# A two-layer attention decoder on one core: small TensorE work handed out between the big matmuls, attention units one per step, memory loads on a second queue

## The chip, the cores and the metric

One core of a Trainium2 chip runs the whole program. The metric is the device time in microseconds, median of three runs. TensorE (PE) multiplies; its weight loads stand in the profile as an engine of their own, PEld. ScalarE (ACT) and VectorE (DVE) read the products, GpSimd (POOL) works on SBUF only, SyncE (SP) issues nearly all transfers. In the matmul rows, "128*128 128x512" is an array use of 128 rows by 128 columns and a moving operand of 512 columns.

## What is computed

256 tokens of width 1024 pass two layers. Each layer normalises, projects, attends in three ways and merges. All is float32.

```python
for l in range(2):
    h = rmsnorm(x, norm_g[l]); z = h @ w_in[l]              # 1024 -> 7968
    o_a = nsa(nsa_q, nsa_kv, gate, compress weights) * silu(nsa_silu)   # 8 heads of 64, 2 kv groups
    o_b = fox(fox_qkv, fox_f, ...) * silu(fox_silu)                     # 8 heads of 64, forget gate
    o_m = memory_xattn(mem_q, rmsnorm(mem) @ w_mem_kv[l]) * silu(mem_silu)   # 4 heads of 128
    u = g0 * (o_a @ w_branch_a) + g1 * (o_b @ w_branch_b) + g2 * (o_m @ w_branch_m)
    x = x + u @ w_out[l]
```

## The kernel before

**Big matmuls.** Every weight matrix is streamed in pieces of 256 rows by up to 512 columns (`stream`). `load_w` issues a piece's transfer into `wraw` (4 buffers); `split_w` splits it into a high part on ACT (L168) and a low part on DVE (L169), 3 buffers each. `gemm_steps` (L233 to L235) multiplies one piece: for two token blocks and two row blocks three matmuls of 512 columns (high*high, low*high, high*low), 12 in all; this is a **step**, and a projection has four. `silu_path_T` (L769 to L772) is a step with 24 matmuls of 256 columns. A projection accumulates in PSUM banks of the tag "mm" (3 buffers). The projections run in the order `ORDER`.

**Small work.** After each step `tick()` advances a clock. Everything that follows a projection (norms, rotary embedding, transposes through PSUM tag "T" with 2 buffers, splits of the transposed result) is queued with `later(d, fn)` and traced d ticks on. Attention is cut into **units**: `scores` (matmuls into PSUM tag "S", 2 buffers, then mask, max, exp, sum, and the multiply by 1/sum on POOL, L496), one `unit_step` later `transpose` (L502), one later `product` (L453, into tag "O", 1 buffer). A layer has 4 + 8 NSA units (`Unit` in `nsa_units`, token block 0 and 1), a `Cmp` unit after each of these two groups (the compressed branch, L879 and L911), 8 fox units (L1043, L1045) and 4 memory units (L1109). A unit starts only when its `deps` are marked, and a unit that may not start blocks the units behind it. `tick()` makes four unit steps.

**The narrow matmuls.** `compress_in` (L662) gathers the compress rows with 8 float32 products of a 128x64 weight against a 64-column selector, twice a layer; the trace shows each as two instructions. `compress_out` (L793 and on) has a few more narrow ones. `compress_step` runs between the steps of FK and takes an "S" bank for two steps.

**Order.** A scheduler of the language, with a timeline of its own, lays out each engine's instructions: what is traced earlier goes first, once it is ready on that timeline. The engines then run that order.

**The start.** 8 matmuls on zeros (`WARM`, L275), the gains' transpose (L297), the transposes of the memory's first quarter of columns (L363), then the first step of memory keys. SP issues, in this order, memory quarter 0, weight piece 0 in two halves, quarter 1, piece 1, quarter 2, piece 2, quarter 3, then x.

Of the kernel before, what the change touches and what calls it, by code (L numbers as in the profile page):

```python
# [26 lines left out]
WARM = 8  # L27

ORDER = "K2 K1 Q SA SB FK MG FQ FV SM MQ".split()
# [30 lines left out]
def hybrid_kernel(ctx: ExitStack, tc, I, cst_d, out_d):  # L60
# [131 lines left out]

    def tick():
# [23 lines left out]
    def need(k):  # L217
        for _ in range(60):
            if k in done_:
                return  # L220
            tick()
        raise AssertionError(k)

    def gemm_steps(act, pp, g, last, consume):
# [29 lines left out]
    def mem_cols(mrow, g):  # L254

        cs = slice(g * 256, (g + 1) * 256)
        nc.sync.dma_start(mrow[:, :, cs], I["mem"][0].rearrange("(t p) d -> p t d", p=128)[:, :, cs])
# [8 lines left out]
    for g in range(4):  # L266
        mem_cols(mrow0, g)
# [80 lines left out]
    def to_T(dst, src, t, k0, scale=1.0):  # L348

        hi, lo = dst[:2]  # L350
        q = pT()
        for k in range(4):
            nc.tensor.transpose(q[:, k * 128:(k + 1) * 128], src[:, k * 128:(k + 1) * 128], ident)
        ts = slice(t * 128, (t + 1) * 128)
        split_evac(hi[:, k0:k0 + 4, ts], lo[:, k0:k0 + 4, ts], q.rearrange("p (k t) -> p k t", k=4), scale)

    def to_T_scaled(dst, src, g, gain):

        hi, lo = dst[:2]
        q = pT()  # L360
        for k in range(2):
            for t in range(NT):
                nc.tensor.transpose(q[:, (k * 2 + t) * 128:(k * 2 + t + 1) * 128],  # L363
                                    src(t)[:, (g * 2 + k) * 128:(g * 2 + k + 1) * 128], ident)
        for k in range(2):
            kg, s = g * 2 + k, q[:, k * 256:(k + 1) * 256]
            gc = gain[:, kg:kg + 1]
            nc.scalar.activation(hi[:, kg, :], s, AF.Copy, scale=gc)
            nc.vector.scalar_tensor_tensor(lo[:, kg, :], s, gc, hi[:, kg, :].bitcast(F32), op0=ALU.mult, op1=ALU.subtract)  # L369
# [13 lines left out]
    def mem_load():  # L383
        mrow = S([128, NT, D], "big")
        for g in range(4):
            mem_cols(mrow, g)
        return mrow

    def mem_norm(l, mrow):

        mT = act_pair(8, "aT")
        for g in range(4):
            def f(g=g):
                to_T_scaled(mT, lambda t: mrow[:, t, :], g, gk[:, l * 8:l * 8 + 8])
                if g == (3 if l else 0):
                    mark("mem")
# [4 lines left out]
            else:  # L401
                f()
        return mT
# [10 lines left out]
    def mem_kv(l, mT, rm):  # L414
# [3 lines left out]
        def on_k(t, p):  # L418
# [3 lines left out]
            def s1():  # L422
# [3 lines left out]
                def s2():  # L426
                    q = pT()
                    for h in range(4):
                        nc.tensor.transpose(q[:, h * 128:(h + 1) * 128], kn[:, h * 128:(h + 1) * 128], ident)
                    ts = slice(t * 128, (t + 1) * 128)  # L430
                    split_evac(KT[0][:, :, ts], KT[1][:, :, ts], q.rearrange("p (h t) -> p h t", h=4))
# [12 lines left out]
    class Out:  # L444
# [4 lines left out]
        def add(self, cols, lhsT, rhs):  # L449
            first = self.O is None  # L450
            if first:
                self.O = pO()
            nc.tensor.matmul(self.O[0:lhsT.shape[1], cols], lhsT, rhs, start=first, stop=False, skip_group_check=True)  # L453

        def close(self):
            self.left -= 1
            if self.left == 0:
                self.done(self.O)

    class Unit:  # L460
# [9 lines left out]
        def scores(self):  # L470
            sp = pS()
            self.score(sp)
# [26 lines left out]
        def transpose(self):  # L499
            q = pT()  # L500
            for i, b in enumerate(self.order):
                nc.tensor.transpose(q[:, i * 128:(i + 1) * 128], self.P[:, b * 128:(b + 1) * 128], ident)  # L502
            w = 128 * len(self.order)
            self.PT = [S([128, 512], tag, bufs=2, dt=F32R)[:, :w] for tag in ("PTh", "PTl")]
            split_evac(self.PT[0], self.PT[1], q[:, :w])
# [24 lines left out]
    for l in range(2):  # L530
# [76 lines left out]
        def rope_k(t, p, i):  # L607
# [4 lines left out]
            def s1():  # L612
                nc.vector.tensor_tensor(kr, kr, b3(r, 2, 64), op=ALU.mult)

                def s2():
                    q = pT()
                    nc.tensor.transpose(q[:, 0:128], kr.rearrange("p h d -> p (h d)"), ident)
# [7 lines left out]
                    mark(("k", l, i, t))  # L625
                later(2 + t, s2)
# [30 lines left out]
        def compress_in(i):  # L657
            q = pT()
# [13 lines left out]
            def s1():  # L672
                nc.scalar.activation(Lhl[i][:, :, 0:30], L3, AF.Copy)
                nc.vector.tensor_tensor(Lhl[i][:, :, 30:60], L3, Lhl[i][:, :, 0:30].bitcast(F32), op=ALU.subtract)
            later(1, s1)
        def run_k2():
# [43 lines left out]
        def on_q(t, p):  # L720
# [4 lines left out]
            def s1():  # L725
# [5 lines left out]
                def s2():  # L731
                    q = pT()
                    for j in range(4):
# [462 lines left out]
```

## Time and profile before

| | us |
|---|---|
| three runs | 645.84, 646.88, 647.96 (median 646.88) |
| the profiled execution | 646.12 |
| its span, first to last instruction | 644.30 |
| TensorE busy in the span | 627.9 (97%) |
| VectorE busy | 485.3 (75%) |
| ScalarE busy | 391.6 (61%) |
| mean granted clock, share of 2.4 GHz | 0.996 |

Ends of matmuls are modelled, and neighbours overlap, so what a matmul costs is read from the distance of its start to the next start. "[1.97 <-DVE sg L754]" behind a row means that the engine was idle for 1.97 us before it, and what ended the idleness.

### The profile page before, as it was taken

How to read it: one execution, taken by the hardware profiler on the slowest of the kernel's cores; microseconds unless marked ns; L12 is line 12 of the kernel's file. 1: busy time of each engine (PE TensorE's matmuls, PEld its weight loads, DVE VectorE, ACT ScalarE, POOL GpSimd, SP SyncE). 2: the span in 40 equal slices, each digit the busy share in tenths (PEclk: the TensorE clock that was granted, in tenths of full speed). 3: DMA queues.
4: the chain of work that ended last, by engine and by line, in shares of the span. 5: the costliest groups of instructions: out<-in, count | busy, mean ns of one | idle time of the engine just before them, and what ended most of it. 6: DMA issues, size and time to landing. Idle time of an engine off the chain costs nothing.

```text
span 644.3 us, 10311 instructions
## 1 busy us (share of the span) xinstructions
PE 627.9 (97%) x3567; PEld 538.3 (84%) x3567; DVE 485.3 (75%) x849; ACT 391.6 (61%) x822; POOL 173.7 (27%) x232
## 2 busy tenths in 40 slices
PE   7999999999998999999999999999999899999997
PEld 5699997878997888888888989877889788888885
DVE  3678889958986976946677798996799588776463
ACT  5767558655756766544557656785566566665441
POOL 1813403343412310603003141140053032052030
PEclk9999999999999999999999999999999999999999
DMA  8757654865343545445655665656544345545541
GB/s 298 182 151 230 195 159 140 198 201 148 121 131 101 161 142 153 134 162 196 229 179 140 191 194 162 172 156 198 160 127 139 91 134 162 163 131 152 175 161 69
DMA packets 75412, 104.51 MB, mean 162 GB/s; under 512 B 16832, under 2 KB 31456, under 8 KB 75360
## 3 DMA queue, kind: packets, MB, share of 16 engines
q1 hardware_dynamic: 75296, 103.84, 54.7%
q8 instruction: 28, 0.46, 0.3%
q14 instruction: 24, 0.20, 0.1%
q10 hardware_dynamic: 64, 0.02, 0.0%
HBM read 102.78 MB, written 1.05 MB: 161 GB/s over the span
## 4 chain that ended last, share of the span: by engine, by line
PE 91%; DVE 3%; DMA 3%; ACT 1%; issue 1%; SPq 0%; ACTq 0%
PE mm L235 20%; PE mm L233 20%; PE mm L234 20%; PE mm L769 4%; PE mm L771 4%; PE mm L772 4%; PE O L453 3%; PE T L502 3%; PE S L235 2%; PE S L233 2%; PE S L234 2%; DMA wraw<-in_w_mem_kv_dram 1%; DVE wlo L169 1%; DMA big<-in_mem_dram 1%; PE S L1109 1%
## 5 line engine op out<-in xcount | busy, mean ns | idle before, releaser
L169 DVE TENSOR_TENSOR wlo<-wraw,whi 128x1024 fp32r<-128x1024 f32 (+3 forms) x185 | 234.2, 1268 | 96.6 <-ACT whi L168 92.0
L168 ACT ACTIVATE whi<-wraw 128x1024 fp32r<-128x1024 f32 (+3 forms) x185 | 192.0, 1039 | 129.3 <-PE mm L234 66.6
L233 PE MATMUL mm<-whi,aTh 128*128 128x512 f32 (+1 forms) x480 | 190.4, 400 | 4.7 <-DVE sg L754 3.9
L234 PE MATMUL mm<-whi,aTl 128*128 128x512 f32 (+1 forms) x480 | 189.4, 395 | 0.1
L235 PE MATMUL mm<-wlo,aTh 128*128 128x512 f32 (+1 forms) x480 | 184.0, 397 | 2.0 <-DVE wlo L169 2.0
L496 POOL TENSOR_TENSOR P<-P,d 128x512 f32<-128x512 f32 (+1 forms) x64 | 57.3, 909 | 197.6 <-DVE d L492 84.5
L233 PEld LDWEIGHTS mm<-whi,aTh 128*128 128x128 f32 x480 | 90.9, 190 | 22.2 <-DVE sg L754 4.7
L235 PEld LDWEIGHTS mm<-wlo,aTh 128*128 128x128 f32 x480 | 90.8, 190 | 20.1 <-DVE wlo L169 3.7
L234 PEld LDWEIGHTS mm<-whi,aTl 128*128 128x128 f32 x480 | 91.2, 190 | 17.3 <-DVE aTl L369 1.1
L769 PE MATMUL mm<-aTh,whi 128*128 128x256 f32 x192 | 54.8, 286 | 0.0
L771 PE MATMUL mm<-aTl,whi 128*128 128x256 f32 x192 | 54.7, 285 | 0.0
L772 PE MATMUL mm<-aTh,wlo 128*128 128x256 f32 x192 | 54.2, 284 | 0.0
L485 ACT ACTIVATE P<-S,m 128x256 f32<-128x256 f32 (+1 forms) x112 | 47.0, 429 | 9.1 <-DVE m L482 6.4
L1019 POOL TENSOR_TENSOR big<-big,t 128x512 f32<-128x512 f32 x16 | 30.0, 1893 | 60.6 <-DVE t L1018 60.6
L339 ACT ACTIVATE PTh<-T 128x512 fp32r<-128x512 f32 (+1 forms) x48 | 26.9, 563 | 22.8 <-PE T L502 22.3
L233 PE MATMUL mm<-whi,oTh 128*128 128x512 f32 x96 | 38.7, 405 | 0.0
L234 PE MATMUL mm<-whi,oTl 128*128 128x512 f32 x96 | 38.3, 399 | 0.0
L235 PE MATMUL mm<-wlo,oTh 128*128 128x512 f32 x96 | 37.7, 396 | 0.0
L769 PEld LDWEIGHTS mm<-aTh,whi 128*128 128x128 f32 x192 | 36.7, 191 | 0.5
L771 PEld LDWEIGHTS mm<-aTl,whi 128*128 128x128 f32 x192 | 36.6, 191 | 0.2
L772 PEld LDWEIGHTS mm<-aTh,wlo 128*128 128x128 f32 x192 | 36.5, 191 | 0.2
L482 DVE TENSOR_REDUCE m<-S 128x2 f32<-128x512 f32 (+3 forms) x64 | 32.6, 514 | 1.0 <-ACT P L485 0.7
(248 smaller groups left out, 1022.3 us busy)
## 6 DMA issues: line engine op xcount, KB each, us to landing
wraw<-in_w_in_dram SPq DMA_DIRECT2D x112, 512.0 KB, 3.7
wraw<-in_w_out_dram SPq DMA_DIRECT2D x16, 512.0 KB, 3.9
wraw<-in_w_mem_kv_dram SPq DMA_DIRECT2D x15, 512.0 KB, 5.1
wraw<-in_w_branch_a_dram SPq DMA_DIRECT2D x16, 256.0 KB, 4.0
wraw<-in_w_branch_b_dram SPq DMA_DIRECT2D x8, 512.0 KB, 3.6
wraw<-in_w_branch_m_dram SPq DMA_DIRECT2D x8, 512.0 KB, 3.6
wraw<-in_w_in_dram SPq DMA_DIRECT2D x8, 408.0 KB, 3.4
wraw<-in_w_in_dram SPq DMA_DIRECT2D x8, 384.0 KB, 3.6
```

The costliest lines, as they stand in the source:

```text
L168: nc.scalar.activation(wh[:, j, :n], v[:, j, :n], AF.Copy)
L169: nc.vector.tensor_tensor(wl[:, j, :n], v[:, j, :n], wh[:, j, :n].bitcast(F32), op=ALU.subtract)
L233: nc.tensor.matmul(o_, hi[:, kg, ts], wh[:, k, :n], start=(kg == 0), stop=False)
L234: nc.tensor.matmul(o_, lo[:, kg, ts], wh[:, k, :n], start=False, stop=False)
L235: nc.tensor.matmul(o_, hi[:, kg, ts], wl[:, k, :n], start=False, stop=last and k == 1)
L482: nc.vector.tensor_reduce(m[:, n:n + c], heads(sp[:, o_:o_ + w * c], c), axis=AXX, op=ALU.max, negate=True)
L485: nc.scalar.activation(self.P[:, k], sp[:, k], AF.Exp, bias=m[:, n:n + 1], accum_out=d[:, n:n + 1])
L496: nc.gpsimd.tensor_tensor(P3, P3, b3(d[:, n:n + c], c, w), op=ALU.mult)
L769: nc.tensor.matmul(o_, ch, hi[:, kg, :], start=(kg == 0 and j % 2 == 0), stop=False, skip_group_check=True)
L771: nc.tensor.matmul(o_, ch, lo[:, kg, :], start=False, stop=False, skip_group_check=True)
L772: nc.tensor.matmul(o_, cl, hi[:, kg, :], start=False, stop=(kg == 7), skip_group_check=True)
L1019: nc.gpsimd.tensor_tensor(uv, uv, tn, op=ALU.add)
```

## The change

- `ORDER` becomes K2 K1 Q SA SB FK FQ FV MG SM MQ: the first merge gate MG moves behind FQ and FV.
- `tick()` makes one unit step in place of four, and a unit step traces scores, then products, then transposes.
- Small matmuls and transposes are not traced at once: `put` collects them in the list `small`, and after each big matmul `hand_out` takes the list's share, so that it is spread evenly over the 12 (or 24) matmuls of the next step. `issue_after` holds what is handed out behind that big matmul in TensorE's order. The last piece of a group brings what reads its result (softmax, split, fold). What is left is traced at the next tick (`flush`).
- So handed out are: all transposes, all scores, all products, and the eight products of `compress_in`. Marks are set when the last piece is traced.
- The two `Cmp` units of a layer come after all 12 NSA units.
- `WARM` is 4 in place of 8. Memory quarters 1 to 3 of the first layer are issued from ScalarE's queue, quarter 0 and the second layer's from SP's.
- `compress_step` first waits (in tracing) for the rows it needs.

```diff
-WARM = 8
-ORDER = "K2 K1 Q SA SB FK MG FQ FV SM MQ".split()
+WARM = 4
+ORDER = "K2 K1 Q SA SB FK FQ FV MG SM MQ".split()
...
+    def hand_out(left):
+
+        for _ in range(-(-len(small) // left)):
+            small.pop(0)()
+
+    def put(*fns):
+
+        def f():
+            for fn in fns:
+                fn()
+        small.append(f)
...
     def tick():
+        flush()
         clock[0] += 1
-        for _ in range(4):
-            unit_step()
+        unit_step()
...
         pipe[1], pipe[0] = t_, None
-        if t_:
-            t_.transpose()
-        if p_:
-            p_.product()
         if units and done_.issuperset(units[0].deps):
             u_ = units.pop(0)
             u_.scores()
             pipe[0] = u_
+        if p_:
+            p_.product()
+        if t_:
+            t_.transpose()
...
-                nc.tensor.matmul(o_, hi[:, kg, ts], wh[:, k, :n], start=(kg == 0), stop=False)
-                nc.tensor.matmul(o_, lo[:, kg, ts], wh[:, k, :n], start=False, stop=False)
-                nc.tensor.matmul(o_, hi[:, kg, ts], wl[:, k, :n], start=False, stop=last and k == 1)
+                for i, (a, w_) in enumerate(((hi, wh), (lo, wh), (hi, wl))):
+                    mi = nc.tensor.matmul(o_, a[:, kg, ts], w_[:, k, :n], start=(kg == 0 and i == 0),
+                                          stop=(last and k == 1 and i == 2))
+                    if small:
+                        with tc.issue_after(mi.ins):
+                            hand_out(12 - t * 6 - k * 3 - i)
...
-        mem_cols(mrow0, g)
+        mem_cols(mrow0, g, nc.scalar if g else nc.sync)
...
-            for g in range(2):
-                for t in range(NT):
-                    for a in range(2):
-                        nc.tensor.matmul(q[a * 64:(a + 1) * 64, g * 128 + t * 64:g * 128 + (t + 1) * 64],
-                                         kcr[:, t, i, g, :], sel[a], start=True, stop=True)
+            for j, gta in enumerate(todo):
+                put(lambda gta=gta: one(*gta), *([lambda: compress_rows(i, q[0])] if j == len(todo) - 1 else []))
...
-        for t in range(NT):
-            units.extend(nsa_units(t))
+        nu_ = [u_ for t in range(NT) for u_ in nsa_units(t)]
+        units.extend(sorted(nu_, key=lambda u_: isinstance(u_, Cmp)))
```

## Rows read from the trace of the kernel before

**Rows 1.** The page's first two parts: TensorE's busy time, share and instructions, and the granted clock in 40 slices of the span.
```profile
PE 627.9 (97%) x3567; PEld 538.3 (84%) x3567; DVE 485.3 (75%) x849; ACT 391.6 (61%) x822; POOL 173.7 (27%) x232
...
PEclk9999999999999999999999999999999999999999
```

**Rows 2.** What TensorE's matmuls waited for: who, us in total, times, longest.
```profile
PE mm L233 <- DVE sg L754: 3.9, 2, 2.0
...
PE mm L235 <- DVE wlo L169: 2.0, 5, 0.5
...
PE T L502 <- DVE PTl L341: 1.0, 2, 0.5
```

**Rows 3.** Timeline of TensorE around a run of four transposes: start, us, instruction.
```profile
262.70 0.40 PE L235 MATMUL mm<-wlo,oTh 128*128 128x512 f32 x1
262.93 0.60 PE L502 MATMUL T<-cst,P 128*128 128x128 f32 x4
...
263.60 0.39 PE L234 MATMUL mm<-whi,oTl 128*128 128x512 f32 x1
263.83 0.39 PE L235 MATMUL mm<-wlo,oTh 128*128 128x512 f32 x1
```

**Rows 4.** The same around one transpose that stands alone.
```profile
58.01 0.39 PE L234 MATMUL mm<-whi,aTl 128*128 128x512 f32 x1
58.23 0.27 PE L617 MATMUL T<-cst,t 128*128 128x128 f32 x1
...
58.59 0.40 PE L233 MATMUL mm<-whi,aTh 128*128 128x512 f32 x1
```

**Rows 5.** The same around one unit's scores, four matmuls of 256 columns between two big ones.
```profile
151.28 0.39 PE L234 MATMUL mm<-whi,aTl 128*128 128x512 f32 x1
151.51 0.28 PE L942 MATMUL S<-KH,big 128*128 128x256 f32 x1
...
152.22 0.40 PE L233 MATMUL mm<-whi,aTh 128*128 128x512 f32 x1
```

**Rows 6.** Timeline of all engines where the first layer's MQ should begin.
```profile
195.72 1.06 PE L911 MATMUL O<-eT,Vc 128*128 128x128 f32 x8
...
196.62 1.03 PE L1045 MATMUL S<-aTl,aTh 65*128 65x256 f32 x4
196.82 0.69 DVE L922 TENSOR_TENSOR o<-o,O 128x512 f32<-128x512 f32 x1 [3.88 <-PE O L911]
...
198.89 0.68 DVE L754 SCALAR_TENSOR_TENSOR sg<-sq,mm 128x512 f32<-128x512 f32 x1
...
199.62 0.50 PE L233 MATMUL mm<-whi,aTh 128*128 128x512 f32 x1 [1.97 <-DVE sg L754]
```

**Rows 7.** A stretch behind the second layer's copy of that place: start:end, length, busy time of PE, PEld, DVE, ACT, POOL with instructions, granted clock, DMA share, GB/s.
```profile
512.60:516.05 3.45, 3.45 (x10) 2.68 (x9) 2.11 (x6) 2.27 (x7) 1.90 (x4) 0.51 0.00 0
```

**Rows 8.** Timeline of all engines at the start.
```profile
1.50 3.78 PE L275 MATMUL S<-P 128*128 128x512 f32 x8 [1.50 <-DVE P L272]
...
2.26 0.43 SPq L257 DMA_DIRECT2D big<-in_mem_dram  x1
...
6.92 0.47 ACT L368 ACTIVATE aTh<-T,gk 128x256 fp32r<-128x256 f32 x1 [0.93 <-DVE gk L298]
...
8.98 1.09 PE L363 MATMUL T<-cst,big 128*128 128x128 f32 x4 [2.42 <-DMA big<-in_mem_dram]
...
9.72 1.20 PE L233 MATMUL mm<-whi,aTh 128*128 128x512 f32 x2
10.72 0.63 PE L234 MATMUL mm<-whi,aTl 128*128 128x512 f32 x1
...
11.15 0.63 PE L235 MATMUL mm<-wlo,aTh 128*128 128x512 f32 x1
```

**Rows 9.** Transfers issued at 2.2 to 2.4 us: into what, from where, by whom, how many, KB each, us from issue to landing.
```profile
big<-in_mem_dram SPq DMA_DIRECT2D x1, 256.0 KB, 6.6
```

**Rows 10.** Timeline of TensorE around a run of `compress_in` (eight narrow products, 16 instructions).
```profile
83.51 0.28 PE L772 MATMUL mm<-aTh,wlo 128*128 128x256 f32 x1
83.72 0.69 PE L662 MATMUL T<-cst,Vc 128*64 128x64 f32 x16
...
84.56 0.28 PE L771 MATMUL mm<-aTl,whi 128*128 128x256 f32 x1
```

**Rows 11.** The same around a narrow float32 instruction that stands alone.
```profile
134.96 0.39 PE L235 MATMUL mm<-wlo,aTh 128*128 128x512 f32 x1
135.28 0.27 PE L793 MATMUL T<-cst,cmph 60*128 60x60 f32 x1
...
135.81 0.40 PE L234 MATMUL mm<-whi,aTl 128*128 128x512 f32 x1
```

**Rows 12.** Timeline of VectorE: the last input of K1's key transposes.
```profile
64.65 0.29 DVE L613 TENSOR_TENSOR t<-t,rk 128x128 f32<-128x128 f32 x1
```

**Rows 13.** Timeline of TensorE, 74.5 to 94.3 us, without the big matmuls: forget gate (L708), K1's keys (L617), the queries (L734), the first scores (L942).
```profile
75.78 0.39 PE L708 MATMUL T<-cst,lf 128*8 128x128 f32 x2
...
76.53 0.33 PE L617 MATMUL T<-cst,t 128*128 128x128 f32 x1
...
88.51 0.60 PE L734 MATMUL T<-cst,t 128*128 128x128 f32 x4
93.98 0.28 PE L942 MATMUL S<-KH,big 128*128 128x256 f32 x1
```

**Rows 14.** Line L942 in 140 to 182 us, the eight NSA units of block 1 (two a unit): duration min/median/max in ns, first and last start, form.
```profile
L942 PE MATMUL S<-KH,big x16: 277/280/364, 146.4 to 175.3; 128*128 128x256 f32 x16
```

More of the change, by code (lines that the diff above doesn't have):

```diff
@@ L191, in later, with flush, put_T, one @@
         conts.append((clock[0] + d, fn))
+    small = []
+    def flush():
+        while small:
+            small.pop(0)()
+    def hand_out(left):
+        for _ in range(-(-len(small) // left)):
+            small.pop(0)()
+    def put(*fns):
[3 more added lines that the diff above has]
+        small.append(f)
+    def put_T(blocks, then):
+        q = []
+        def one(i, b):
+            if i == 0:
+                q.append(pT())
+            b = b()
+            nc.tensor.transpose(q[0][0:b.shape[1], i * 128:(i + 1) * 128], b, ident)
+        for i, b in enumerate(blocks):
+            put(lambda i=i, b=b: one(i, b), *([lambda: then(q[0])] if i == len(blocks) - 1 else []))
     def tick():
+        flush()
         clock[0] += 1
-        for _ in range(4):
-            unit_step()
+        unit_step()
         due = [c for c in conts if c[0] <= clock[0]]
@@ L402, in mem_norm @@
                 f()
+                flush()
         return mT
@@ L449, in add, with f @@
         def add(self, cols, lhsT, rhs):
[L450 to L453, printed above, removed]
+            def f():
+                first = self.O is None
+                if first:
+                    self.O = pO()
+                nc.tensor.matmul(self.O[0:lhsT.shape[1], cols], lhsT, rhs, start=first, stop=False,
+                                 skip_group_check=True)
+            put(f)
         def close(self):
@@ L470, in scores, with bank, softmax @@
         def scores(self):
-            sp = pS()
-            self.score(sp)
+            box = []
+            def bank():
+                if not box:
+                    box.append(pS())
+                return box[0]
+            self.score(bank)
+            mm = small.pop()
+            put(mm, lambda: self.softmax(box[0]))
+        def softmax(self, sp):
             if self.diag:
@@ L499, in transpose, with out @@
         def transpose(self):
[L500 to L502 removed]
             w = 128 * len(self.order)
[L504 to L505 removed]
+            def out(q):
+                self.PT = [S([128, 512], tag, bufs=2, dt=F32R)[:, :w] for tag in ("PTh", "PTl")]
+                split_evac(self.PT[0], self.PT[1], q[:, :w])
+            put_T([lambda b=b: self.P[:, b * 128:(b + 1) * 128] for b in self.order], out)
         def product(self):
@@ L729, in s1, with out @@
                                             op=ALU.mult)
-                def s2():
-                    q = pT()
-                    for j in range(4):
-                        nc.tensor.transpose(q[:, j * 128:(j + 1) * 128], qp[:, j].rearrange("p g d -> p (g d)"), ident)
+                def out(q):
                     q = q.rearrange("p (j t) -> p j t", j=4)
@@ L742, in s2 @@
                     mark(("q", l, t))
-                later(1 + t, s2)
+                later(1 + t, lambda: put_T([lambda j=j: qp[:, j].rearrange("p g d -> p (g d)") for j in range(4)], out))
             later(1, s1)
@@ L768, in silu_path_T @@
                         ch, cl = [w_[:, k, j * 128:(j + 1) * 128] for w_ in (wh, wl)]
-                        nc.tensor.matmul(o_, ch, hi[:, kg, :], start=(kg == 0 and j % 2 == 0), stop=False,
-                                         skip_group_check=True)
-                        nc.tensor.matmul(o_, ch, lo[:, kg, :], start=False, stop=False, skip_group_check=True)
-                        nc.tensor.matmul(o_, cl, hi[:, kg, :], start=False, stop=(kg == 7), skip_group_check=True)
+                        for i, (w_, a) in enumerate(((ch, hi), (ch, lo), (cl, hi))):
+                            mi = nc.tensor.matmul(o_, w_, a[:, kg, :], start=(kg == 0 and j % 2 == 0 and i == 0),
+                                                  stop=(kg == 7 and i == 2), skip_group_check=True)
+                            if small:
+                                with tc.issue_after(mi.ins):
+                                    hand_out(24 - j * 6 - k * 3 - i)
                     if q == 3 and j % 2:
@@ L980, in s1, with out @@
                     nc.vector.tensor_tensor(heads(z, 8), heads(p, 8), b3(r, 8, 64), op=ALU.mult)
-                    def s2():
-                        q = pT()
-                        for j in range(4):
-                            nc.tensor.transpose(q[:, j * 128:(j + 1) * 128], z[:, j * 128:(j + 1) * 128], ident)
+                    def out(q):
                         for e in range(2):
@@ L995, in s2 @@
                             mark(("q" if is_q else "k", l, t, h0))
-                    later(1 + t, s2)
+                    later(1 + t, lambda: put_T([lambda j=j: z[:, j * 128:(j + 1) * 128] for j in range(4)], out))
                 later(1, s1)
@@ L1069, in s1, with out @@
                 nc.vector.tensor_tensor(heads(z, 4), heads(p, 4), b3(r, 4, 128), op=ALU.mult)
-                def s2():
-                    q = pT()
-                    for h in range(4):
-                        nc.tensor.transpose(q[:, h * 128:(h + 1) * 128], z[:, h * 128:(h + 1) * 128], ident)
+                def out(q):
                     ts = slice(t * 128, (t + 1) * 128)
@@ L1077, in s2 @@
                     mark(("mq", l, t))
-                later(1 + t, s2)
+                later(1 + t, lambda: put_T([lambda h=h: z[:, h * 128:(h + 1) * 128] for h in range(4)], out))
             later(1, s1)
```

121 lines of the change are left out of this document (66 added, 55 removed).

## The prediction

> **What bounds the kernel now.** I read the page's busy shares first, then the waits of TensorE, then its timeline at each wait. TensorE is busy 97% of 644.3 us and at the full clock in every slice [rows 1], so there is little idle time to win: its matmuls waited for a few things only, above all twice for VectorE's L754, a few times for weight splits and split transposes [rows 2], and once, at the start, for a memory quarter [rows 8]. The rest is the stream itself. A 512-column matmul starts 0.23 us after the one before it (263.60 to 263.83) [rows 3], so a step of 12 is 2.7 us. The change moves almost no work off TensorE. It can win the waits, the start, and whatever small work costs by where it stands; it can lose by the same.
>
> **Does small work get cheaper between big matmuls?** A run of four transposes: 262.70 to 263.60 is 0.90, less two big matmuls of 0.23, so 0.44, or 0.11 each [rows 3]. One alone: 58.01 to 58.59 is 0.58, less 0.46, so 0.12 [rows 4]. Four score matmuls in a run: 0.94 less 0.46, so 0.12 each [rows 5]. So a transpose gains nothing by standing alone; to the printed hundredth it loses 0 to 0.02. A unit has about 16 pieces (4 scores, 4 transposes, 8 products): 1.9 us. A layer has 14 NSA and compressed, 8 fox and 4 memory units, some 350 pieces, 700 in all. Sixteen pieces on twelve matmuls go out two at a time at first and then singly, and many stand alone already (rows as [rows 4] are frequent), so I take 250 pieces newly alone at 0.01: **+2.5 us**, bounds 0 and 250 x 0.02 = 5.
>
> **The two stalls at MQ.** At 196.62 TensorE has four passes of fox scores; by their busy time of 1.03 they are over by 197.65 (modelled ends reach 0.15 past the point at which a successor could start, 0.40 - 0.23 in rows like those of [rows 3]), and the next matmul starts at 199.62 [rows 6]. It needs a bank of "mm", which SM still holds until L754 has read it; L754 is behind the Cmp unit's L922 and L924 in VectorE's order, and L922 idles VectorE for 3.88 us because TensorE reaches L911 only at 195.72 [rows 6]. So a loss of 2.1, in both layers (3.9 us recorded in two waits [rows 2]). In the changed order the Cmp units come at FQ and FV, the fox units at MG, and during SM and MQ no unit starts, so nothing of this queues in front of L754. What is late next is a Cmp product of the same kind at FQ or FV: behind it in VectorE's order stand the weight splits L169, and with two pieces split ahead TensorE has 2 x 2.7 us of cover against 3.9, so I let it cost nothing; without the cover it is again up to 2 us a layer. **-4.2 us**, bounds -4.4 and 0.
>
> **The clock.** Behind the second of these stalls TensorE ran 3.45 us at 0.51 of its clock [rows 7], that is the 1.2 GHz level; half of it is lost. If the stall goes, this goes: **-1.7 us**. In the first layer the same stall left the clock alone [rows 1], so it hangs on more than the stall, and I keep 0 as the other bound.
>
> **The start.** Eight zero matmuls run 1.50 to 5.28; the memory's second transposes wait until 8.98 for quarter 1, and only then comes the first real matmul, at 9.72, though its input aTh was written from 6.92 [rows 8]. Quarter 1 was issued at 2.26 and landed 6.6 us later [rows 9]. With the change its transposes are handed out behind the second half of step 0, so step 0 can begin at about 6.92 + 0.47 + 0.1 = 7.5: 2.2 us earlier. This is the upper bound of the gain. Against it: the weight pieces still come off the same transfers, now with three quarters beside them; and each quarter's transposes now end three matmuls before the step that needs them (0.7 us), while the copy alone is 0.47 and there are two on each engine, so 0.3 to 0.5 is lost in each of three steps. I take **-1.0 us**, bounds -2.2 and +0.5. The four zero matmuls less are off the path: they end before aTh is there either way. The matmuls at 10.72 and 11.15 stand 0.43 apart [rows 8], twice the 0.23 of [rows 3], so step 0 runs at half speed behind the pause of 2.42; I let step 0 stay at that speed.
>
> The trace shows all bulk transfers competing in one stretch. The Trainium skill, "DMA: Bandwidth & Descriptors", part on arbitration, says that each DMA engine takes turns between the queues that have work, packet by packet; by this rule the quarters on their own queue get half of the bandwidth early and the weight pieces come later. No row before shows two loaded queues, so the trace neither agrees nor speaks against it; what it would do is rival 5.
>
> **Waits for weight splits and split transposes.** L169 and L341 ended 2.0 + 1.0 us of waits in seven places [rows 2], mostly in FK, where four units, the compress matmuls and twice as many weight splits meet. In the changed order up to 10 units meet there, one per step, so I take 0 and keep -3.0 and the rival below.
>
> **The narrow products.** A run of eight (`compress_in`) takes 83.51 to 84.56 less two of 0.12, so 0.81 us, 0.10 each [rows 10]. A narrow float32 instruction alone between big ones takes 134.96 to 135.81 less 0.46, so 0.39 [rows 11]: entering and leaving costs most of it. 32 of them handed out singly would be 32 x 0.39 - 4 x 0.81 = 9.2 us more. But the bounds of hand_out are only lower ones, and I expect the runs to stay: K1's key transposes had their input at 64.65 plus 0.29 [rows 12] and ran at 76.53, right behind the forget gate's products at 75.78, which stand before them in the order of "T" banks [rows 13]. That gate is untouched, so `compress_in`, next in the same order, is late against its step again, and all eight are free when their bank comes. So 0, bounds 0 and +9.2.
>
> **Sum.** 646.1 (the profiled execution: 644.3 span and 1.8 around it) - 4.2 - 1.7 - 1.0 + 2.5 = 641.7. The profiled execution stands 0.8 under the median of 646.9, so 642.5 for the median.
>
> **Rivals.**
> 1. *Narrow products alone.* If the "T" banks come in time, each of the 32 pays 0.39: 642.5 + 9.2 = 651.7. For it: the pieces are laid one behind each matmul. Against it: the late "T" banks of [rows 12, 13]. The Trainium skill, "TensorEngine Tiling (Array Packing)", Key Properties, states that a change of tiling mode drains TensorE; [rows 10, 11] agree with it, and it speaks against this part of the change.
> 2. *The units dam up before FK* (slower). The first scores ran at 93.98, since the queries' transposes came at 88.51 [rows 13]. By the changed clock the first unit belongs two steps into SA, so at SB's end six are overdue, and the compress bank of "S" now stands behind seven units instead of four. Eight units took 28.9 us in 7.5 distances, 3.9 each [rows 14], so the seventh scores at 94 + 6 x 3.9 = 117. Until then TensorE has two FK steps (5.5), six units (11.4), and about 1.2 of narrow products and transposes: 5 us idle, against 1.5 now; +3.5 in each layer, 649.5. It decides when a unit takes over about 3.0 us in this stretch: then 6 x 3.0 equals TensorE's 18.
> 3. *The stall moves.* Cmp's late product blocks VectorE elsewhere and TensorE waits as before: 642.5 + 4.2 + 1.7 = 648.4. The change then doesn't do what it is for; the cover of two pieces speaks against it.
> 4. *All waits go.* The start gains its 2.2 and the splits' 3.0 vanish: 642.5 - 1.2 - 3.0 = 638.3. For it: spreading cuts the bursts on VectorE (75% busy [rows 1]).
> 5. *The quarters crowd the weights.* Quarters 1 to 3 are as many bytes (768 KB) as one and a half weight pieces. If they come in front of pieces 1 and 2 and not between them, the step that is gained at 7.5 is waited for at step 1: the start's 1.0 goes, and up to 0.5 more: 642.5 + 1.5 = 644.0. For it: quarter 1 alone took 6.6 us [rows 9]. Against it: the quarters were needed for these steps anyway.
>
> **How the numbers follow.** Forecast 0.38, rival 1 0.10, rival 2 0.20, rival 3 0.10, rival 4 0.16, rival 5 0.06. Differences under 0.3% (1.9 us) can't be told from none here. Faster by more (under 645.0): rival 4, and most of the forecast and of rival 5, 0.54. Slower by more (over 648.8): rivals 1 and 2 without their mild ends, and a little of rival 3, 0.27. The rest, rival 3 above all, 0.19. The range leaves out half of rival 1 and the low end of rival 4: 637.5 to 650.5. Faster cases alone reach from 637.5 to 645.
>
> **What would show it.** After: the wait for L754 gone from TensorE's waits; no stretch at half clock late in the span; the first real matmul near 7.5; L662 still x16 in one row of the timeline (alone: 16 rows of 0.2 to 0.4 apart); the compress products L858 begun well before 117; transposes alone at 0.12. I am wrong if TensorE's idle time in FK grows, or if its busy stream itself grows by more than 3 us.

## The result, and the profile after

The changed kernel takes **655.96 us** (median of 4: 654.90 to 656.83) against 646.39 of the kernel before beside it. The record's ratio of the runs is 1.0138, interval 1.0122 to 1.0154 (the two medians alone give 1.0148). It was forecast faster, 642.5 with a range to 650.5; it is 9.6 us slower, outside the range and on the other side. The profiled execution took 656.39, its span is 654.7.

The page after, busy line and granted clock; of before, [rows 1] answer:

```profile
PE 631.8 (97%) x3563; PEld 538.9 (82%) x3563; DVE 479.7 (73%) x849; ACT 392.9 (60%) x822; POOL 176.0 (27%) x232
...
PEclk9889999899999999999999999999999999999999
```

TensorE still has 97%, as before: the share of busy time doesn't show the loss. The clock row shows part of it: of 40 slices, the 2nd, 3rd and 8th are below 9, where [rows 1] have none. What TensorE waited for (us in total, times, longest), to lay beside [rows 2]:

```profile
PE mm L266 <- ACT whi L168: 3.6, 3, 1.7
PE mm L266 <- ACT aTh L398: 3.1, 1, 3.1
PE mm L266 <- DVE wlo L169: 1.6, 4, 0.5
PE S L1005 <- ACT P L529: 1.6, 2, 0.8
PE O L485 <- DVE o L558: 1.6, 2, 0.8
...
PE mm L266 <- DVE sg L804: 0.7, 2, 0.4
```

The wait for the gate's product, L754 before and L804 here, fell from 3.9 to 0.7, as was forecast. New are 3.1 + 3.6 for ScalarE, nearly all in the first 40 us, and, in each layer's FK, one wait of 0.8 for ScalarE's exponential (`P`) and one of 0.8 for VectorE's fold (`o`). So there are two places of loss.

**The start.** Timeline of all engines, picked lines ([rows 8] before):

```profile
6.96 0.47 ACT L398 ACTIVATE aTh<-T,gk 128x256 fp32r<-128x256 f32 x1
...
8.01 1.22 PE L266 MATMUL mm<-whi,aTh 128*128 128x512 f32 x2 [1.61 <-ACT whi L168]
...
10.11 0.45 PE L220 MATMUL T<-cst,big 128*128 128x128 f32 x1 [0.88 <-DMA big<-in_mem_dram]
...
13.34 0.41 PE L220 MATMUL T<-cst,big 128*128 128x128 f32 x1
...
14.41 0.63 PE L266 MATMUL mm<-whi,aTl 128*128 128x512 f32 x1
14.84 0.63 PE L266 MATMUL mm<-wlo,aTh 128*128 128x512 f32 x1
...
14.91 1.06 ACT L443 ACTIVATE t<-big 128x1024 f32<-128x1024 f32 x1 [0.83 <-DMA big<-in_mem_dram]
...
15.97 1.04 ACT L443 ACTIVATE t<-big 128x1024 f32<-128x1024 f32 x1
...
17.00 1.04 ACT L633 ACTIVATE t<-x 128x1024 f32<-128x1024 f32 x1
...
18.04 0.45 ACT L398 ACTIVATE aTh<-T,gk 128x256 fp32r<-128x256 f32 x1
...
18.55 0.74 PE L266 MATMUL mm<-whi,aTh 128*128 128x512 f32 x2 [3.08 <-ACT aTh L398]
```

Read it from the end. At 18.55 TensorE has been idle for 3.08 us, waiting for the copy L398 of 18.04. That copy's last transpose stands at 13.34, one of four handed out between matmuls at half speed since 10.11 (14.41 to 14.84 is 0.43, against 0.23 in [rows 3]; the granted clock in the profile's rows reads 1.00 up to 18.5, so this half speed is read from the distances). ScalarE was idle for 0.83 us up to 14.91, but in its order the squares of the memory (L443) come first, and they wait for the last quarter; then three squares run, 3.1 us with the first of x (L633), and only then the copy. About 1 us behind the pause TensorE is at half clock. Stretches as windows (start:end, length, busy time of PE, PEld, DVE, ACT, POOL, granted clock, DMA share, GB/s):

```profile
121.70:125.00 3.30, 3.09 (x15) 2.29 (x13) 3.20 (x6) 1.59 (x5) 2.08 (x2) 0.51 0.02 9
19.50:22.50 3.00, 3.00 (x9) 1.78 (x7) 2.28 (x4) 1.34 (x3) 2.79 (x5) 0.50 0.39 31
36.80:40.00 3.20, 3.20 (x8) 2.56 (x9) 2.06 (x4) 0.85 (x5) 1.68 (x4) 0.52 0.53 136
...
506.00:540.00 34.00, 34.00 (x224) 30.68 (x223) 26.77 (x56) 24.35 (x69) 8.07 (x17) 1.00 0.51 138
```

The last row is the second layer's SM and MQ, where the stall and the stretch of [rows 7] were: busy throughout, at the full clock. The first three are at the 1.2 GHz level, each behind idle time; half of their length, some 4.7 us in all, is lost, more than in the one of [rows 7]. A second pause at 35.54 is of a similar make: the weight split L168 stands on ScalarE behind squares (L366) that wait for a step's last matmul:

```profile
33.03 0.37 ACT L366 ACTIVATE sq<-mm,rm 128x128 f32<-128x128 f32 x1 [2.17 <-PE mm L266]
...
34.42 1.06 ACT L168 ACTIVATE whi<-wraw 128x1024 fp32r<-128x1024 f32 x1
...
35.54 0.50 PE L266 MATMUL mm<-whi,aTh 128*128 128x512 f32 x1 [1.71 <-ACT whi L168]
```

The loss of the start in one row each, 15 to 40 us, first of the kernel before, then of the changed one: 112 TensorE instructions against 76. If all were of the 0.23 us of [rows 3], the 36 would be 8.3 us; some are transposes, so it is an upper estimate.

```profile
15.00:40.00 25.00, 23.62 (x112) 18.08 (x111) 16.31 (x24) 18.32 (x42) 15.33 (x38) 1.00 0.70 184
```

```profile
15.00:40.00 25.00, 19.19 (x76) 13.91 (x75) 12.50 (x19) 15.28 (x38) 14.19 (x37) 0.86 0.63 150
```

**FK.** The compress products (L858 before, L911 after) and the NSA scores in front of them (L942 before, L1005 after), in 90 us and on: duration in ns, first and last start. Before, eight such matmuls, two a unit, so four units; after, sixteen, so eight units:

```profile
L858 PE MATMUL S<-whi,oTh x16: 221/222/225, 106.3 to 108.9; 128*60 128x128 f32 x16
...
L942 PE MATMUL S<-KH,big x8: 277/280/282, 94.0 to 101.3; 128*128 128x256 f32 x8
```

```profile
L911 PE MATMUL S<-whi,oTh x16: 221/223/227, 125.8 to 127.8; 128*60 128x128 f32 x16
...
L1005 PE MATMUL S<-KH,big x16: 277/280/384, 97.2 to 121.6; 128*128 128x256 f32 x16
```

Compress begins at 125.8 instead of 106.3. Of these 19.5 us some 9 come from the start. The rest is the row of units. Most of that is work which only comes earlier than before: four more units, by the prediction's 1.9 us a unit some 7.6 us. What is lost is the time in which TensorE waits for one unit's exponential and another's fold, and the half clock behind it (the window 121.7 above):

```profile
119.12 0.38 PE L1005 MATMUL S<-KH,big 128*128 128x256 f32 x1 [0.81 <-ACT P L529]
...
120.64 0.39 PE L485 MATMUL O<-PTh,VN 128*128 128x256 f32 x1 [0.78 <-DVE o L558]
...
122.85 2.34 PE L220 MATMUL T<-cst,P 128*128 128x128 f32 x8
```

Why eight? In the queue of units only the head is tested. Before, the first Cmp unit stood fifth and needs `kc` and `vc`, which compress makes: it held back everything behind it. Sorted to the end, it holds back nothing.

Two things came as forecast: the narrow products stay in runs of eight, all four of them (one is below; before, [rows 10]), and a transpose alone costs 0.12 (27.51 to 27.86 is 0.35, less 0.23; as [rows 4]):

```profile
27.51 0.27 PE L220 MATMUL T<-cst,t 128*128 128x128 f32 x1
27.54 0.48 PE L266 MATMUL mm<-whi,aTl 128*128 128x512 f32 x1
27.86 0.27 PE L220 MATMUL T<-cst,t 128*128 128x128 f32 x1
...
86.50 0.69 PE L709 MATMUL T<-cst,Vc 128*64 128x64 f32 x16
```

### The profile page after: what moved, and what is told of

Same layout as the page of the kernel before. It is cut to its first block, busy times and chain, and to the rows that moved or that the text cites. A ratio compares the mean times of both kernels' runs of the same rounds, so it can differ in the third digit from the quotient of the medians.

```text
span 654.7 us, 10288 instructions
## 1 busy us (share of the span) xinstructions
PE 631.8 (97%) x3563; PEld 538.9 (82%) x3563; DVE 479.7 (73%) x849; ACT 392.9 (60%) x822; POOL 176.0 (27%) x232
## 4 chain that ended last, share of the span: by engine, by line
PE 81%; DVE 10%; ACT 3%; issue 3%; DMA 2%; POOL 0%; ACTq 0%; DVEq 0%; POOLq 0%
PE mm L266 57%; PE S L266 6%; PE T L220 5%; PE mm L820 5%; DVE wlo L169 3%; PE O L485 3%; DMA big<-in_mem_dram 2%; ACT whi L168 1%; PE S L1104 1%; DVE m L526 1%; DVE S L520 1%; PE S L1164 1%; DVE PTl L376 1%; DVE sg L804 1%; DVE big L790 1%
## 5 line engine op out<-in xcount | busy, mean ns | idle before, releaser
L169 DVE TENSOR_TENSOR wlo<-wraw,whi 128x1024 fp32r<-128x1024 f32 (+3 forms) x185 | 227.3, 1230 | 95.5 <-ACT whi L168 91.4
L168 ACT ACTIVATE whi<-wraw 128x1024 fp32r<-128x1024 f32 (+3 forms) x185 | 192.3, 1040 | 113.4 <-PE mm L266 81.2
L540 POOL TENSOR_TENSOR P<-P,d 128x512 f32<-128x512 f32 (+1 forms) x64 | 55.5, 879 | 180.0 <-DVE d L532 143.6
L529 ACT ACTIVATE P<-S,m 128x128 f32<-128x128 f32 (+1 forms) x112 | 47.0, 433 | 8.7 <-DVE m L526 4.9
L1078 POOL TENSOR_TENSOR big<-big,t 128x512 f32<-128x512 f32 x16 | 31.8, 2005 | 69.4 <-DVE t L1077 69.4
L374 ACT ACTIVATE PTh<-T 128x512 fp32r<-128x512 f32 (+1 forms) x48 | 27.0, 563 | 19.1 <-PE T L220 18.5
L526 DVE TENSOR_REDUCE m<-S 128x1 f32<-128x128 f32 (+2 forms) x64 | 32.7, 515 | 1.4 <-PE S L1164 1.0
```

Source lines behind the costliest of these rows:

```text
L168: nc.scalar.activation(wh[:, j, :n], v[:, j, :n], AF.Copy)
L169: nc.vector.tensor_tensor(wl[:, j, :n], v[:, j, :n], wh[:, j, :n].bitcast(F32), op=ALU.subtract)
L374: nc.scalar.activation(hi, src, AF.Copy, scale=scale)
L526: nc.vector.tensor_reduce(m[:, n:n + c], heads(sp[:, o_:o_ + w * c], c), axis=AXX, op=ALU.max, negate=True)
L529: nc.scalar.activation(self.P[:, k], sp[:, k], AF.Exp, bias=m[:, n:n + 1], accum_out=d[:, n:n + 1])
L540: nc.gpsimd.tensor_tensor(P3, P3, b3(d[:, n:n + c], c, w), op=ALU.mult)
```

## The experiments

All times are medians; the ratio, with its interval, is the record's, to the kernel before on the same chip. The e runs start from the changed kernel, the b runs from the kernel before; what each edits stands below. From each trace, which is one execution, four times in us: the first silu matmul of the first layer's SA (a measure of the start), the first compress product, the first silu matmul of the second layer's SA; and the span. e12's trace is of an execution of 642.48, below its median.

| kernel | us | ratio (interval) | SA | compress | SA, second layer | span |
|---|---|---|---|---|---|---|
| before | 646.39 | | 67.0 | 106.3 | 379.2 | 644.3 |
| changed | 655.96 | 1.0138 (1.0122 to 1.0154) | 76.3 | 125.8 | 391.5 | 654.7 |
| e1 | 651.36 | 1.0058 (1.0035 to 1.0081) | 70.4 | 119.9 | 385.2 | 649.7 |
| e2 | 649.28 | 1.0035 (1.0022 to 1.0048) | 68.5 | 117.9 | 383.2 | 646.4 |
| e3 | 649.67 | 1.0048 (1.0033 to 1.0064) | 67.3 | 119.2 | 386.0 | 649.2 |
| b1 | 663.56 | 1.0257 (1.0235 to 1.0279) | 66.8 | 131.4 | 388.8 | 661.0 |
| e4 | 644.12 | 0.9954 (0.9937 to 0.9972) | 69.8 | 105.6 | 382.1 | 642.5 |
| e5 | 649.16 | 1.0030 (1.0015 to 1.0045) | 68.6 | 118.0 | 383.3 | 648.0 |
| e6 | 649.61 | 1.0040 (1.0024 to 1.0057) | 69.6 | 119.1 | 384.8 | 648.0 |
| e7 | 638.85 | 0.9874 (0.9855 to 0.9893) | 69.6 | 105.3 | 379.5 | 637.5 |
| e8 | 656.53 | 1.0154 (1.0128 to 1.0179) | 76.2 | 126.0 | 392.5 | 655.8 |
| e9 | 640.22 | 0.9907 (0.9888 to 0.9926) | 69.0 | 104.8 | 379.4 | 638.3 |
| b2 | 640.96 | 0.9919 (0.9901 to 0.9938) | 66.7 | 106.0 | 376.9 | 638.8 |
| e10 | 639.17 | 0.9893 (0.9874 to 0.9911) | 66.6 | 105.4 | 379.6 | 637.4 |
| e11 | 649.87 | 1.0048 (1.0033 to 1.0063) | 70.8 | 120.2 | 385.5 | 649.8 |
| e12 | 644.82 | 0.9970 (0.9953 to 0.9987) | 72.9 | 108.7 | 382.9 | 640.8 |

### The start: e1, e2, e3, e8, e11

**e1**, the quarters back on SyncE's queue:

```
-        mem_cols(mrow0, g, nc.scalar if g else nc.sync)
+        mem_cols(mrow0, g, nc.sync)
```

> The changed kernel with the memory's quarters 1 to 3 back on SyncE's queue, all else as changed. Theory A (TensorE's start is late because the transposes of quarter 1 are handed out behind step 0's second half, so that their copies stand behind the squares L443 and L633 in ScalarE's order): the order stays, so the idle time of about 3 us at 18.5 stays too, and the time is 655 to 656. Theory B (the quarters on ScalarE's queue are the cause: the second half of piece 0 lands after 7.0 us instead of 3.5, the activation table is loaded behind three issues, the last quarter lands at 14.9 instead of 13.1): the first real matmul comes 1 to 2 us earlier and the time is 647 to 650.

**e2**, the memory's transposes at once:

```
-                within.append(f)
+                within.append(lambda f=f: (f(), flush()))
```

> The changed kernel, but the first layer's memory transposes are laid down at once between the halves of a step instead of being handed out behind its second half; the quarters stay on ScalarE's queue, four matmuls on zeros stay. Theory A: the copies of quarter 1 stand in front of the squares again, so the idle 3.1 us at 18.5 go, with the half-clock stretch behind them (about 1.5) and part of the next one at 35.5 (1.7 idle and 1.5 of half clock): 649 to 652. Theory B: 655 to 656, since the landings stay late.

**e3**, both, and `WARM = 8`.

> The changed kernel with the whole start of before: quarters on SyncE's queue, eight matmuls on zeros, the memory transposes of the first layer laid down at once. If the start is what the change loses (A and B together, 8.5 us up to 40 us of the span), 647 to 648. If the loss is spread over the kernel as small work alone between matmuls, 653 or more.

e2 gave 649.3, as theory A said, with the quarters still on ScalarE's queue; in 15 to 40 us TensorE has 109 instructions again. So with the transposes at once the queue does no harm. But e1, with the transposes still handed out, gave 651.4: it missed theory A's forecast and came close to theory B's, and its first real matmul came 1.3 us sooner, as theory B said. Its rows:

```profile
6.68 1.22 PE L266 MATMUL mm<-whi,aTh 128*128 128x512 f32 x2 [0.67 <-ACT aTh L398]
...
15.29 0.45 ACT L398 ACTIVATE aTh<-T,gk 128x256 fp32r<-128x256 f32 x1
...
15.80 0.73 PE L266 MATMUL mm<-whi,aTh 128*128 128x512 f32 x2 [1.54 <-ACT aTh L398]
```

The pause did not stay at 3.08 but fell to 1.54, and not for the transfers' sake alone: in ScalarE's order the copy had moved in front of the squares of x (15.29, and those squares from 15.65). How much of it the landing makes, e12 (below) shows, which has the changed kernel's start: in its trace the squares of the memory begin at 12.78, 2.1 us sooner than in the changed kernel, and yet the pause is as long.

```profile
12.78 1.06 ACT L443 ACTIVATE t<-big 128x1024 f32<-128x1024 f32 x1 [0.39 <-DMA big<-in_mem_dram]
...
16.43 1.22 PE L266 MATMUL mm<-whi,aTh 128*128 128x512 f32 x2 [3.06 <-ACT aTh L398]
```

So in these traces the length of this pause goes with the squares that stand in front of the copy, three there and two in e1; a late landing moves it to a later time. Either edit, e1 or e2, takes away most of the loss, so the loss needs both the handed-out transposes and the start with the second queue. e3 is no better than e2, so with the transposes at once neither the queue nor the four matmuls on zeros matter; 2 us of the 8.5 that were expected to go stayed. In e2 ScalarE's order reads:

```profile
9.10 0.84 ACT L398 ACTIVATE aTh<-T,gk 128x256 fp32r<-128x256 f32 x2 [1.21 <-PE T L220]
...
10.77 0.47 ACT L398 ACTIVATE aTh<-T,gk 128x256 fp32r<-128x256 f32 x1
...
12.49 1.04 ACT L443 ACTIVATE t<-big 128x1024 f32<-128x1024 f32 x1
```

Quarter 1's copies are out at 11.2, and the squares run under steps 0 and 1.

**e8** turns that order round (the squares of x are held behind the last copy in the same way, and with `norm_x` they come a tick later):

```
+    rm = [None, None]
+    def stats0():
+        with tc.issue_after(copied[-1].ins):   # the last copy L398 so far
+            rm[:] = mem_stats(mrow0)
+    later(2, stats0)
...
-        later(1, norm_x)
+        later(1 if l else 2, norm_x)           # its squares behind the copy too
```

> The changed kernel (656.0) with one thing of the start turned round: in ScalarE's order the squares of the memory and of x (L443, L633) stand behind the copies of quarter 1 instead of in front of them. Quarters on ScalarE's queue, four matmuls on zeros and the handing out stay. Theory A in its narrow form (it is the order on ScalarE, not the late transposes as such): the idle 3.1 us at 18.55 and the half clock behind it go, 650 to 652, near e2 (649.3). If late handing out costs by itself, 654 to 656.

656.5, over both forecasts. The 3.08 us went, and came back elsewhere. The edit went further than its text: the last copies when the squares are traced are those of quarter 2 (17.64 and 19.42 in this trace), not of quarter 1 (13.20 and 14.98). The squares now run from 19.79, the norm of x from 27.70, and TensorE waits for x; the pause at 35.5 is there too, with the half clock behind it:

```profile
19.79 1.05 ACT L443 ACTIVATE t<-big 128x1024 f32<-128x1024 f32 x1
...
22.82 1.05 ACT L639 ACTIVATE t<-x 128x1024 f32<-128x1024 f32 x1
...
27.70 0.75 DVE L641 TENSOR_SCALAR t<-x,rx 128x1024 f32<-128x1024 f32 x1 [2.87 <-POOL rx L355]
...
28.60 0.30 PE L220 MATMUL T<-cst,t 128*128 128x128 f32 x1 [1.79 <-DVE t L641]
```

So squares that stand too late cost as much as squares that stand too early: an order is only as good as the room for it. Theory A's narrow form, that the order alone is to blame, is neither shown nor refuted by it, since squares right behind quarter 1's copies were not run. **e11** makes the room:

```
-                nc.scalar.activation(xn[t], x[t], AF.Square, accum_out=ss)
+                nc.gpsimd.memset(ss, float(D))   # first layer; L443 likewise
```

> The changed kernel (656.0) without the squares L443 and L633 of the first layer at all: the sums are set to the width, so the first layer's norms of the memory and of x are left out of the computation; everything else of the start is as changed. If the squares in ScalarE's order are the whole loss of the start (theory A, narrow), TensorE's lag at 40 us is as in e2, about 11, and the time 648 to 650. If the transposes handed out late hold up the weight splits by themselves (the copy of a handed-out transpose, and the squares L366, standing in front of a split on ScalarE), the lag at 40 us is still 15 to 17 and the time 652 to 655.

649.9, as the narrow form has it. ("Lag" is how far TensorE is behind its work.) In its trace, of an execution of 651.5, TensorE has 99 instructions in 15 to 40 us against 109 in e2, some 2 us; the pause <- whi L168 is there as in the changed kernel, the longest 1.7. By the medians e11 is 0.6 slower than e2, so without the 4.2 us of squares the late transposes cost little. Together: the squares must run somewhere between the landing of the memory and the norm of x. Laid at once, the transposes let the copies out before that; handed out between half-speed matmuls the last of them comes at 13.3, and the squares stand in the way of the copies, or the copies in the way of the squares.

### Units and the stalls at MQ: b1, b2, e4, e6, e7, e9

**b1**, the kernel before with the order and the Cmp units at the end; **b2**, with the order alone:

```
-ORDER = "K2 K1 Q SA SB FK MG FQ FV SM MQ".split()
+ORDER = "K2 K1 Q SA SB FK FQ FV MG SM MQ".split()
...
+        units.extend(sorted(nu_, key=lambda u_: isinstance(u_, Cmp)))   # b1 only
```

> The kernel before with two things of the change alone: the order FK FQ FV MG SM MQ, and the Cmp units behind the other NSA units. Nothing is handed out, four unit steps a tick and the start stay as before. If these two take away the stalls at MQ by themselves, 640 to 642 (two stalls of 2.1 and the half-clock stretch of 1.7). If the twelve NSA units in a row hold up the compress products in FK as in the changed kernel (+2.2 and +2.9 there), 645 to 646.

> The kernel before (646.5) with the new order FK FQ FV MG SM MQ alone; Cmp units in place, nothing handed out, four unit steps a tick. If the order alone is enough against the stalls at MQ, 640.5 to 642 (two stalls of 2.1, a half-clock stretch of 1.7). If not, 646 to 647; if FQ and FV right behind FK crowd the units, above 648.

b1 was slower than either theory had it, 663.6: all twelve NSA units stand before the compress bank, compress begins at 131.4, and TensorE waited 5.7 us for P and 3.9 for GpSimd. b2 gave 641.0: the order alone takes the stalls away, at the size that the prediction had (5.9 forecast, 5.3 measured). But not for its reason. In b2 the second Cmp unit's product and its two folds still come as MQ begins, and in VectorE's order in front of L754, as in [rows 6]:

```profile
194.30 1.05 PE L911 MATMUL O<-eT,Vc 128*128 128x128 f32 x8
...
195.39 0.69 DVE L922 TENSOR_TENSOR o<-o,O 128x512 f32<-128x512 f32 x1
...
196.66 0.68 DVE L924 SCALAR_TENSOR_TENSOR o<-o,sg 128x512 f32<-128x512 f32 x1
...
197.53 0.67 DVE L754 SCALAR_TENSOR_TENSOR sg<-sq,mm 128x512 f32<-128x512 f32 x1
...
198.25 0.50 PE L233 MATMUL mm<-whi,aTh 128*128 128x512 f32 x1
```

The product comes 1.4 us sooner (195.72 before), L922 no longer idles VectorE, L754 is 1.4 us sooner too, and up to 198.25 TensorE has fox scores to do. MQ still goes on right behind the end of L754. Why the new order brings the product sooner stays open.

Between b1 and b2 lies only the place of the Cmp units: 22.6 us.

**e4**, e2 with four units at most before the compress bank:

```
+        nu_.sort(key=lambda u_: isinstance(u_, Cmp))
+        for u_ in nu_[4:]:
+            u_.deps = u_.deps + [("cb", l)]     # marked where compress takes its bank
```

> The kernel of e2 (649.3), and only four NSA units may start before the compress matmuls have their bank of "S"; the others wait until then. If the units in front of that bank are what FK loses (rival 2 of the prediction: between 80 and 130 us e2 falls behind by 6.6 us against 3.6 before, in the second layer 6.3 against 4.0), these 5 us go: 643.5 to 645.5. If FK loses because one unit is started in a step and the units come too late or too thick in any case, the loss moves behind FK: 648 to 650.

644.1, and compress at 105.6: rival 2's mechanism is shown, and its price of 3.5 a layer was somewhat high for the bank alone (5.2 in both layers together, 2.6 in each). **e7**, e2 with the Cmp units in place (`units.extend(nu_)`):

> The kernel of e2 (649.3) with the Cmp units where they were before, each behind its block's NSA units. The first Cmp unit then waits for kc and vc and holds all later units until compress is over, so fewer units stand before the compress bank (four, as before). If rival 2 is right, FK's 5 us go here too: 644 to 646; and if the Cmp units' place took away the stalls at MQ, 4 of these are lost again: 648 to 650.

638.85, below every forecast: 10.4 under e2, and the stalls at MQ stay away. e4 keeps four units back, but lets them come all together afterwards, and TensorE waits 1.5 us for one of them (T <- POOL P) in each layer. The Cmp unit in place holds them until compress is wholly through. That this is the rest of the 10.4, 5.3, is argued from these waits and not tested by itself. What e7 still waits for is above all 3.1 us at the start for a memory quarter, 1.1 for the splits L169 and 1.0, in three waits, for L804.

**e6** is e2, **e9** is e7 with the order of before.

> The kernel of e2 (649.3) with the order of before, FK MG FQ FV SM MQ. If the new order is what took away the stalls at MQ (the units end before SM), they come back: 2.1 in each layer and perhaps the half-clock stretch, 653 to 655. If the handing out or the Cmp units at the end did it, 649; FK itself should not change, since the order differs behind it only.

> The kernel of e7 (638.9) with the order of before, FK MG FQ FV SM MQ. e6 kept that order without stalls at MQ, e7 kept the Cmp units' place without stalls. If handing out takes them away, neither matters: 639 to 640. If it takes one of the two (new order or Cmp units at the end), the stalls come back here: 643 to 645.

Neither brought the stalls back (649.6 and 640.2; no wait for L804 above 0.4). So against these stalls either is enough, the order (b2) or what the rest of the change does to the units (e9); of both together no run shows a further gain beyond 1.4 us (e7 to e9, on two chips).

### Sum and best: e12, e10, and a miss, e5

**e12**, the changed kernel with only that one line, `units.extend(nu_)`:

> The changed kernel with one line taken back: the Cmp units stand where they were before; the start stays as changed. If the two losses add up (the start 6.7 by e2, the Cmp units at the end 10.4 by e2 against e7), 656.0 - 10.4 = 645.6, within 1 us. If the late start also fed the crowd before FK, less is lost here: 647 or more.

644.8, 11.1 less, within the 1 us: the two losses add up. **e10**, e7 with the start of before:

> The kernel of e7 (638.9) with the whole start of before as in e3 (quarters on SyncE's queue, eight matmuls on zeros). e2 and e3 gave the same time, with the lag of TensorE at 40 us 11.3 and 11.0; e7's is 12.4. So 637.5 to 639. It is the candidate that beats both kernels: what is left of the change is the handing out, one unit a step and the order.

639.2, as e7 (0.2 over its forecast). Either beats the kernel before by 1.1 to 1.3%, and the changed one by 2.6%. Beside b2, which has the same start and order but hands nothing out, e10 is 1.8 us faster.

**e5**, e2 with the normed x transposed at once:

```
-later(3 + g, lambda g=g: to_T_scaled(hT, ...))
+later(3 + g, lambda g=g: (to_T_scaled(hT, ...), flush()))
```

> The kernel of e2 (649.3), and the transposes of the normed x are laid down at once in both layers. In e2 ScalarE waits 2.40 us at 341.30 for a run of these transposes, and behind the copy stand the squares of mem_kv and a weight split for which TensorE then waits. If this is theory A's mechanism again (a copy in ScalarE's order waits for transposes handed out late), the 1.1 us at 344.3 and 345.5 go: 648. If it is only the squares, 649.3 as in e2.

649.2, nothing: the loss at the second layer's start is not the handing out of x. Its two waits (0.26 for L168, 0.52 for L169) are there in e2, e5, e7 and e10 and not in b2; what makes them stays open.

## Why the prediction was wrong

**The stalls at MQ (-4.2) and the clock behind them (-1.7)** were right in place and size: b2 has the order alone and gained 5.3. The reason was right only in part, so the size is partly luck. "During SM and MQ no unit starts" is false: in the changed kernel fox scores (L1102, L1104) run from 188.4 to 222, all through SM and MQ. Its Cmp products come at 187.5 and 193.5, well in front of L804 at 206.4, but as MG ends and SM begins, not at FQ and FV. And in b2, e7 and e9 the Cmp unit's folds stand right in front of L754 or L804 as before, without a stall.

**The start (-1.0, bounds -2.2 and +0.5)** is the term that failed, by sign and by far: +9.3 at SA's first silu matmul in the trace, and 6.7 in the time by e2. Its first half was right, the first real matmul came at 8.01 (7.5 was forecast; the split of the first weight half stood behind the copy on ScalarE). The step that failed is "each quarter's transposes now end three matmuls before the step that needs them", for which "0.3 to 0.5 is lost" was put down. It priced the copy as if ScalarE were free when the transposes end. Nothing in the sum asked what stands in front of the copy on ScalarE: 4.2 us of squares run there in the trace of before as in this one, and in the changed kernel three of the four stand in front of quarter 1's copy, so TensorE idles 3.08 us. Each of two repairs, the transposes at once (e2) and no squares (e11), gives 6 to 7 us back; the quarters on SyncE's queue (e1), where one square less stands there, give 4.6.

**The units (0 in the sum, rival 2 at 0.20)** were the second error, of weight and not of mechanism. Rival 2 said seven units before the compress bank, the seventh's scores at 117 and +3.5 a layer; the trace has eight, compress at 125.8 behind a start 9.3 late, and 5.2 a layer for the Cmp units at the end (e2 to e7, 10.4 in two), where the sum had 0. What was missed is that the sort by Cmp is a part of the change by itself, which takes away the brake on the queue; the prediction gives it no term.

**Small work alone (+2.5, bounds 0 and 5)** is not borne out. A transpose alone costs what the prediction said, but the handing out as a whole, one unit a step with it, gains 1.8 (b2 to e10). No run separates the lone pieces from the rest of it. The waits for the splits L169 are 2.0 in b2 and 1.1 in e10, so they can make half of it.

**Narrow products (0)** and rival 1: as forecast, they stay in runs.

**Rival 3** (the stall moves) did not happen. **Rival 4** (all waits go) did not happen in the changed kernel; e7 is near its time (638.85 against 638.3), but by other terms. **Rival 5** is not shown. In the changed kernel the two halves of piece 0 took 5.7 us to land against 3.5 before, and quarters 1 to 3 took 9.8 against 7.7 (medians); but in e2, with the same queues, 3.8 and 7.5, and in e1, with one queue, 3.7 and 7.6. Over all ten profiles with two queues the halves lie between 3.8 and 5.7 and the quarters between 7.5 and 9.8. The Trainium skill, "DMA: Bandwidth & Descriptors", part on arbitration, would have two loaded queues share each DMA engine in turns; the changed kernel's profile agrees in the weights' delay, e2's does not, so no run here shows it.

In one sum: e7's 638.85, and 10.4 for the Cmp units at the end, and 6.7 for the memory's transposes handed out, are 655.95. Both terms are differences of the same medians, so the sum closes by itself; what tests it is e12, forecast at 645.6 from the 10.4 and measured at 644.8. Of the signs that the prediction named for being wrong, both came: TensorE idles more in FK, and its busy time grew by 3.9 us (631.8 against 627.9 [rows 1]).

## What to carry to other kernels

Work that is handed out in pieces ends when its last piece does, so before spreading anything ask which instruction reads the result, on which engine, and what stands in front of that reader in its order. A queue of which only the head is tested has brakes in it: see which entry holds back the rest, and what it was protecting, before sorting. A change of five parts wants five terms, each with a run of its own: here two lines taken back, the sort of the Cmp units and the handing out of the memory's transposes, turn 1.4% slower into 1.3% faster (e7).

## What the runs showed of the hardware

Whether a pause is followed by the 1.2 GHz level can differ between executions. The changed kernel and e12 have the same start, and both wait 1.7 us for whi L168. Behind that wait (35.54) the changed kernel ran at 0.52 (the window from 36.80 above); e12's profiled execution ran on at the full clock:

```profile
33.42 0.50 PE L266 MATMUL mm<-whi,aTh 128*128 128x512 f32 x1 [1.70 <-ACT whi L168]
```

```profile
34.68:37.20 2.52, 2.52 (x10) 1.86 (x11) 1.59 (x4) 0.85 (x6) 1.67 (x4) 1.00 0.53 147
```

Ten runs of e12 fall into two groups: 642.47 and 642.48 at a mean granted clock of 0.997, and eight from 644.75 to 645.39 at 0.990 to 0.995; the profiled execution is of the first group. e11 does the same (six from 648.81 to 649.90 at 0.997, four from 651.26 to 652.06 at 0.992 to 0.995); its profiled execution is of the second group and has a half-clock stretch behind the same wait (0.53 in 31.6 to 34.9). So, with not an instruction changed, some 2 us go with the granted clock, and these two traces fit one half-clock stretch more or less; of the other executions there is no trace. The clock is not all of the spread: e2's runs, at 0.997 to 0.999, still lie 2.9 us apart.
